# Attention scores from high and low parts of queries and keys, in a one-core hybrid decoder layer

## The chip, the core and the metric

The kernel runs on one NeuronCore of a Trainium2 chip. A core has engines that run their own instruction lists in order and wait for one another by semaphores: TensorE (PE, matrix products into PSUM), VectorE (DVE), ScalarE (ACT), GpSimd (POOL) and SyncE (SP, which here issues DMAs). A product has two records in the profile: the load of its stationary operand (PEld) and the product itself (PE). The metric is the device time of one execution, in microseconds (us); lower is better. The kernel before takes 1095.87 us (median of three runs, 1095.17 to 1096.69).

## The reference, cut to what matters

One layer of a decoder for 512 tokens of width 1024: a normalised input goes through three mixers side by side (a state-space mixer, dilated window attention, multi-scale pooling), then a gated sum, an output product and a squared-ReLU feed-forward part. All inputs are float32. The change is in the scores of the attention, of which the reference computes:

```python
# 3 groups of 4 heads, head size 128; group 0 dilation 1, groups 1 and 2 dilation 4 and 16
qh = _rms(q.reshape(b, S, ATTN_HEADS, ATTN_HEAD_DIM).astype(f32), q_norm_w)
kh = _rms(k.reshape(b, S, ATTN_HEADS, ATTN_HEAD_DIM).astype(f32), k_norm_w)
...
s = jnp.einsum('bhdnqe,bhdnke->bhdnqk', qb, kb) * (e ** -0.5)
...
s = jnp.where(valid, s + alibi[:, None, None], -jnp.inf)
lse = jax.nn.logsumexp(s, axis=-1)
```

## The kernel before

**Products.** Big products are not made with float32 operands. A float32 operand is cut into a high part, which ACT writes in the type float32r, and a low part, which DVE writes as the float32 value less the high part. A product is then three products of parts, summed in PSUM: `mm3` (lines 293 to 296) issues weight-high by x-low, weight-high by x-high, weight-low by x-high. `gemm_feat` and `gemm_tok` (lines 298 to 317) run `mm3` over eight blocks of the inner dimension and four accumulators. Their weights come through `wstream` (lines 283 to 291): SP loads a raw tile, ACT writes `wh` from it (line 279), DVE writes `wl` (line 280); four raw tiles and three `wh`, `wl` pairs are in turn.

**The scores.** `scores` (lines 578 to 644) does one group of four heads. For a head, `turn` transposes the four token blocks of queries and of keys on TensorE (lines 592 and 597) into one PSUM bank each, and ACT copies the two banks to `qT` and `kT` in SBUF, the keys scaled by `qkw` (lines 593 and 598). `score` multiplies them as float32 (line 613): four products a head, one for each block of 128 queries, against 128 keys (groups 1 and 2, and the first block of group 0) or 256 keys (the other three blocks of group 0). The profile shows two load and product records for each float32 product. DVE then scales and adds the position table (line 616) and takes maxima, ACT takes exponentials (line 628).

**Order.** The pieces of a group (turn of head 0; turn of head 1 and score of head 0; and so on) are put on a list, and `wstream` calls `tick` once per two blocks of a big product, which takes one piece off. So a head's turn and score stand between the products of the next projection. `flush` takes all pieces that are left at once. The `background` list adds, every second tick, one dot product of the adaLN weights on DVE (line 246) with its two loads on SP (line 240). A scheduler then orders each engine's list by its own estimate of times, with some work put ahead (`tc.high_priority`).

**Memory.** PSUM has eight banks, SBUF tiles of 128x512 come from 49 blocks. Both are handed out by `Slots` (lines 117 to 131): the block that was freed first is taken first, and an instruction that writes a block waits for the readers of its last use. A transposes' bank is free when ACT has copied it.

Of the kernel before, what the change touches and what calls it, by code (L numbers as in the profile page):

```python
# [10 lines left out]
F32 = mybir.dt.float32  # L11
F32R = mybir.dt.float32r
AF = mybir.ActivationFunctionType
ALU = mybir.AluOpType
# [3 lines left out]
P = 128  # L18
# [8 lines left out]
SOON = 200  # L27
# [71 lines left out]
def kernel(ctx: ExitStack, tc: tile.TileContext, a: dict, out: bass.AP, dbg=None):  # L99
    nc = tc.nc  # L100
# [16 lines left out]
    class Slots:  # L117
# [6 lines left out]
        def take(self, name, dt):  # L124
            i = self.idle.pop(0)
            t = self.pool.tile([P, T], dt, tag=f"{self.prefix}{i}", name=uid(name), bufs=1)
            self.used[id(t)] = (i, t)
            return t

        def free(self, t):  # L130
            self.idle.append(self.used.pop(id(t))[0])
# [3 lines left out]
    def blk(name, dt=F32):  # L135
        return sb.take(name, dt)
# [12 lines left out]
    def small(shape, name, bufs=1, dt=F32):  # L149
        return sm.tile(shape, dt, tag=name, name=uid(name), bufs=bufs)  # L150

    def psm(name="m"):
        return banks.take("ps" + name, F32)
# [8 lines left out]
    mm = nc.tensor.matmul  # L162
    V, S = nc.vector, nc.scalar
# [6 lines left out]
    def C(name):  # L170
        at, width = COFF[name]
        return cst[:, at : at + width]

    def table(name):
        at, width = COFF[name]
        t = [blk(name) for _ in range(width // T)]
        for i, x in enumerate(t):
            nc.gpsimd.dma_start(x, a["const"][:, at + i * T : at + (i + 1) * T])
        return t

    ident, tri = C("ident"), C("tri")
# [111 lines left out]
    def mm3(ps, wh, wl, xh, xl, first, last):  # L293
        mm(ps, lhsT=wh, rhs=xl, start=first, stop=False)  # L294
        mm(ps, lhsT=wh, rhs=xh, start=False, stop=False)  # L295
        mm(ps, lhsT=wl, rhs=xh, start=False, stop=last)  # L296
# [44 lines left out]
    with tc.manual_schedule(engines={E.DVE, E.Activation, E.PE, E.SP}):  # L341
# [107 lines left out]
        var, rt, r, t = (small([P, 4], "rx" + n) for n in "vryt")  # L449
# [24 lines left out]
        hl = [cpool.tile([P, T], F32R, name=f"hl{k}", tag=f"hl{k}") for k in range(8)]  # L474
# [31 lines left out]
        qkw = small([P, 1], "qkw")  # L506
# [54 lines left out]
    def take_k(ps):  # L561
        ks, rk = take(ps, "k")
        for tb in range(4):
            kv = ks[tb].rearrange("p (h e) -> p h e", h=4)
            with tc.high_priority(offset=SOON):
                V.tensor_tensor(kv, kv, rk[:, tb * 4 : tb * 4 + 4].unsqueeze(2).broadcast_to([P, 4, P]), ALU.mult)
        return ks
# [4 lines left out]
    def prob_ap(pt, gi, b):  # L572
        if gi == 0:
            n = P if b == 0 else 2 * P
            return pt[b // 2][:, (b % 2 + 1) * 2 * P - n : (b % 2 + 1) * 2 * P]
        return pt[0][:, b * P : (b + 1) * P]

    def scores(gi, qs, rq, ks):

        mx, zs = small([P, 16], f"mx{gi}"), small([P, 16], f"zs{gi}")  # L580
        nmx = small([P, 16], "nmx", 2)
        nkey = 2 * P if gi == 0 else P
        pr, turned, tab = [], {}, []

        def turn(h):
            if h == 0:
                tab.extend(table(f"al{gi}"))
            hs = slice(h * P, (h + 1) * P)
            qT, kT = blk("qT"), blk("kT")
            tp = psm("qT")  # L590
            for tb in range(4):
                nc.tensor.transpose(tp[:, tb * P : (tb + 1) * P], qs[tb][:, hs], ident)  # L592
            S.copy(qT, tp)  # L593
            free(tp)
            tp = psm("kT")
            for tb in range(4):
                nc.tensor.transpose(tp[:, tb * P : (tb + 1) * P], ks[tb][:, hs], ident)  # L597
            S.activation(kT, tp, AF.Copy, scale=qkw)
            free(tp)
            if h == 3:  # L600
                free(*qs, *ks)
            turned[h] = qT, kT

        def score(h):
            qT, kT = turned.pop(h)
            mxh = mx[:, h * 4 : h * 4 + 4]
            al = tab[h * nkey // T][:, h * nkey % T : h * nkey % T + nkey]
            pt = [blk("p") for _ in range(2 if gi == 0 else 1)]
            so, sp = [], [psm("S") for _ in pt]
            for b in range(4):  # L610
                n = prob_ap(pt, gi, b).shape[1]
                so.append(sp[0][:, b * P : (b + 1) * P] if gi else sp[b // 2][:, (b % 2 + 1) * 2 * P - n : (b % 2 + 1) * 2 * P])
                mm(so[b], lhsT=qT[:, b * P : (b + 1) * P], rhs=kT[:, (b + 1) * P - n : (b + 1) * P], start=True, stop=True)  # L613
            for b in range(4):
                ap = prob_ap(pt, gi, b)
                V.scalar_tensor_tensor(ap, so[b], rq[:, b * 4 + h : b * 4 + h + 1], al[:, nkey - ap.shape[1] :], ALU.mult, ALU.add)
                if gi == 0 and b < 2:
                    V.tensor_reduce(mxh[:, b : b + 1], ap, AX, ALU.max)
            free(*sp)
            if gi == 0:  # L620
                V.tensor_reduce(mxh[:, 2:4], pt[1].rearrange("p (b k) -> p b k", b=2), AX, ALU.max)
            else:
                V.tensor_reduce(mxh, pt[0].rearrange("p (b k) -> p b k", b=4), AX, ALU.max)
            nm = nmx[:, h * 4 : h * 4 + 4]
            V.tensor_scalar(nm, mxh, -1.0, None, ALU.mult)
            for b in range(4):
                ap = prob_ap(pt, gi, b)
                S.activation(ap, ap, AF.Exp, bias=nm[:, b : b + 1], accum_out=zs[:, h * 4 + b : h * 4 + b + 1])
            pr.append(pt)
            free(qT, kT)  # L630
            if h == 3:
                free(*tab)

        def piece(h):
            def go():
                if h < 4:
                    turn(h)
                if h > 0:
                    score(h - 1)
            return go  # L640

        probs.append(pr)
        stats.append((mx, zs))
        side.extend(piece(h) for h in range(5))
# [413 lines left out]
    with tc.issue_after(edgeV.ins), tc.issue_after(edgeS.ins):  # L1058
        qs, rq = take(qps, "q")
        ks = take_k(kps)  # L1060
# [3 lines left out]
    for gi in (1, 2):  # L1064
        if gi > 1:
            qps = gemm_tok(w_in, 8, Q + gi, rh, rl)
        qs, rq = take(qps, "q")
        kps = gemm_tok(w_in, 8, K + gi, rh, rl)
        ks = take_k(kps)
# [83 lines left out]
    with tc.manual_schedule(engines={E.DVE, E.Activation, E.PE}):  # L1153
# [61 lines left out]
        ta, tb = halves  # L1215
# [268 lines left out]
```

## Time and profile before

| What | Value |
|---|---|
| Median of three runs | 1095.87 us |
| Profiled execution | 1098.25 us |
| Its span | 1096.5 us, 14976 instructions |
| PE busy | 1087.1 us (99%), 5806 products |
| DVE busy | 717.4 us (65%) |
| ACT busy | 527.8 us (48%) |
| Granted TensorE clock | 1.0 |
| HBM traffic | 121 GB/s over the span |

The times in views are from the start of the span. In a timeline, a row is a run of like instructions on one engine: start, how long from the first start to the last end, engine, line, operation, output and inputs, shape, count. Products are pipelined: a product's record is longer than the time until the next one can start, so what a product costs in a dense row of products is the distance between starts. The chain of waits gives each piece of work only the time by which it held up the end.

### The profile page before, as it was taken

To read this page: it belongs to the slowest core of one execution; us is meant where nothing else is said; L and a number is where in the kernel's file an instruction comes from. 1 tells how busy PE (TensorE), PEld (TensorE's weight loads), DVE (VectorE), ACT (ScalarE), POOL (GpSimd) and SP (SyncE) were. 2 spreads that over 40 slices of the span, in tenths; PEclk is the share of its full clock that TensorE was granted. 3 is DMA by queue.
4 is the path that set the end of the run, shared out by engine and by line. 5 is a ranking of instruction groups with operands and counts; after the bars stand their busy time and mean duration, and the time that the engine had idled before them with its cause. 6 is when DMAs were issued, how large, how long until landed. Compare 5 with 4: busy or idle time off the path is not lost.

```text
span 1096.5 us, 14976 instructions
## 1 busy us (share of the span) xinstructions
PE 1087.1 (99%) x5806; PEld 927.0 (85%) x5806; DVE 717.4 (65%) x1383; ACT 527.8 (48%) x845; POOL 3.6 (0%) x10
## 2 busy tenths in 40 slices
PE   9999999999999999999999999999999999999998
PEld 7878888888887877888888888899889989989987
DVE  8975874582776778568843424577787587686664
ACT  8965875543695536625432123354344334335330
POOL 0000000000000000000000000000000000000000
PEclk9999999999999999999999999999999999999999
DMA  9853342443542354321232325360214224134032
GB/s 349 306 183 98 128 134 86 152 168 102 173 125 87 117 181 136 104 97 58 96 115 97 106 96 163 97 230 1 79 57 154 65 90 136 59 114 135 20 116 77
DMA packets 46666, 133.98 MB, mean 122 GB/s; under 512 B 5362, under 2 KB 6130, under 8 KB 46596
## 3 DMA queue, kind: packets, MB, share of 16 engines
q1 hardware_dynamic: 45392, 130.28, 36.0%
q0 software_dynamic: 480, 1.57, 0.5%
q10 hardware_dynamic: 724, 1.18, 0.3%
q8 instruction: 45, 0.74, 0.3%
q14 instruction: 25, 0.20, 0.1%
HBM read 130.89 MB, written 2.13 MB: 121 GB/s over the span
## 4 chain that ended last, share of the span: by engine, by line
PE 87%; ACT 4%; DVE 3%; DMA 3%; issue 1%; SPq 0%; ACTq 0%; DVEq 0%
PE psacc L294 22%; PE psacc L296 22%; PE psacc L295 22%; PE psacc L1345 11%; PE psacc L534 4%; DMA M<-prow 2%; PE psS L613 1%; DMA wa<-in_w_ada_dram 1%; DVE conv L850 1%; ACT wh L279 1%; PE pso L729 1%; PE pso L727 1%; DVE wl L280 1%; PE pskT L597 0%; PE psqT L592 0%
## 5 line engine op out<-in xcount | busy, mean ns | idle before, releaser
L280 DVE TENSOR_TENSOR wl<-raw,wh 128x1024 fp32r<-128x1024 f32 x140 | 171.0, 1222 | 192.2 <-ACT wh L279 190.9
L279 ACT CAST wh<-raw 128x1024 fp32r<-128x1024 f32 x140 | 146.8, 1050 | 241.1 <-PE psacc L295 168.8
L294 PE MATMUL psacc<-hl,wh 128*128 128x512 f32 x416 | 166.6, 401 | 3.4 <-DVE X L882 2.2
L295 PE MATMUL psacc<-hh,wh 128*128 128x512 f32 x416 | 162.1, 390 | 0.0
L296 PE MATMUL psacc<-hh,wl 128*128 128x512 f32 x416 | 162.0, 390 | 0.0
L295 PE MATMUL psacc<-ah,wh 128*128 128x512 f32 (+1 forms) x260 | 100.4, 386 | 0.0
L294 PE MATMUL psacc<-al,wh 128*128 128x512 f32 (+1 forms) x260 | 100.4, 386 | 0.0
L296 PE MATMUL psacc<-ah,wl 128*128 128x512 f32 (+1 forms) x260 | 100.3, 386 | 0.0
L294 PEld LDWEIGHTS psacc<-hl,wh 128*128 128x128 f32 x416 | 78.2, 188 | 21.7 <-DVE X L882 2.7
L295 PEld LDWEIGHTS psacc<-hh,wh 128*128 128x128 f32 x416 | 78.2, 188 | 16.9 <-issue 1.4
L296 PEld LDWEIGHTS psacc<-hh,wl 128*128 128x128 f32 x416 | 78.1, 188 | 16.7
L294 PE MATMUL psacc<-wl,rh 128*128 128x512 f32 x192 | 76.9, 401 | 0.0
L296 PE MATMUL psacc<-wh,rl 128*128 128x512 f32 x192 | 75.5, 393 | 0.0
L295 PE MATMUL psacc<-wh,rh 128*128 128x512 f32 x192 | 75.3, 392 | 0.0
L296 PEld LDWEIGHTS psacc<-ah,wl 128*128 128x128 f32 x260 | 48.8, 188 | 9.9
L294 PEld LDWEIGHTS psacc<-al,wh 128*128 128x128 f32 x260 | 48.9, 188 | 9.7
L295 PEld LDWEIGHTS psacc<-ah,wh 128*128 128x128 f32 x260 | 48.9, 188 | 9.6
L1405 DVE SCALAR_TENSOR_TENSOR xr<-psacc,modv,xr 128x512 f32<-128x512 f32 (+1 forms) x65 | 44.7, 739 | 18.6 <-PE psacc L296 18.6
L246 DVE SCALAR_TENSOR_TENSOR wa<-wa,crow 128x512 f32<-128x512 f32 x64 | 43.1, 688 | 20.0 <-DMA wa<-in_w_ada_dram 20.0
L296 PEld LDWEIGHTS psacc<-wh,rl 128*128 128x128 f32 x192 | 36.0, 188 | 7.6
L294 PEld LDWEIGHTS psacc<-wl,rh 128*128 128x128 f32 x192 | 36.1, 188 | 7.3 <-ACT qT L593 0.2
L295 PEld LDWEIGHTS psacc<-wh,rh 128*128 128x128 f32 x192 | 36.1, 188 | 7.0
(408 smaller groups left out, 2360.8 us busy)
## 6 DMA issues: line engine op xcount, KB each, us to landing
raw<-in_w_in_dram SPq DMA_DIRECT2D x80, 512.0 KB, 3.5
raw<-in_w_ff_dram SPq DMA_DIRECT2D x52, 512.0 KB, 3.7
wa<-in_w_ada_dram SPq DMA_DIRECT2D x64, 256.0 KB, 3.6
wada<-in_w_ada_dram SPq DMA_DIRECT2D x14, 512.0 KB, 7.8
rawl<-in_w_ff_dram SPq DMA_DIRECT2D x12, 512.0 KB, 3.5
wst<-in_w_in_dram SPq DMA_DIRECT2D x16, 256.0 KB, 7.8
M<-prow SPq DMA_DIRECT2D x16, 256.0 KB, 3.8
raw<-in_w_ssd_out_dram SPq DMA_DIRECT2D x8, 512.0 KB, 3.5
```

The lines of the kernel that those rows point to most:

```text
L246: V.scalar_tensor_tensor(wa[i], wa[i], 1.0, crow[i], ALU.mult, ALU.mult, accum_out=d[:, i : i + 1])
L279: S.copy(wh, raw)
L280: V.tensor_tensor(wl, raw, wh.bitcast(F32), ALU.subtract)
L294: mm(ps, lhsT=wh, rhs=xl, start=first, stop=False)
L295: mm(ps, lhsT=wh, rhs=xh, start=False, stop=False)
L296: mm(ps, lhsT=wl, rhs=xh, start=False, stop=last)
L534: mm(ps[j], lhsT=t[:, j, :], rhs=w, start=first, stop=last)
L613: mm(so[b], lhsT=qT[:, b * P : (b + 1) * P], rhs=kT[:, (b + 1) * P - n : (b + 1) * P], start=True, stop=True)
L727: mm(od, lhsT=vs[kb][:, hs], rhs=pT[b // 2][:, cs : cs + P], start=(b == 0), stop=False, skip_group_check=True)
L729: mm(ov[:, b, :], lhsT=vs[b][:, hs], rhs=pT[0][:, b * P : (b + 1) * P], start=False, stop=(gi == 2 and b == 3), skip_group_check=True)
L1345: mm(o, lhsT=x[:, cs], rhs=y, start=first and k == 0 and j == 0 and n == 0, stop=k == 3 and n == 2, skip_group_check=True)
L1405: V.scalar_tensor_tensor(xT[d][:, ts], p[:, : ts.stop - ts.start], modv[:, 3, d : d + 1], xT[d][:, ts], ALU.mult, ALU.add)
```

## The change

Query and key banks leave by two instructions each: ACT writes the high part in float32r (the query's copy becomes an activation with scale 1.0), and DVE writes the low part, reading the same PSUM bank and the high part. Both are put ahead in the order. Each score block is now `mm3`: three products of parts in place of one float32 product. A head holds four SBUF blocks (`qTh`, `qTl`, `kTh`, `kTl`) in place of two.

```diff
-            qT, kT = blk("qT"), blk("kT")
-            tp = psm("qT")
-            for tb in range(4):
-                nc.tensor.transpose(tp[:, tb * P : (tb + 1) * P], qs[tb][:, hs], ident)
-            S.copy(qT, tp)
-            free(tp)
-            tp = psm("kT")
-            for tb in range(4):
-                nc.tensor.transpose(tp[:, tb * P : (tb + 1) * P], ks[tb][:, hs], ident)
-            S.activation(kT, tp, AF.Copy, scale=qkw)
-            free(tp)
+            qT, kT = ([blk(n + p, F32R) for p in "hl"] for n in ("qT", "kT"))
+            for t, xs, sc in ((qT, qs, 1.0), (kT, ks, qkw)):
+                tp = psm("qT" if xs is qs else "kT")
+                for tb in range(4):
+                    nc.tensor.transpose(tp[:, tb * P : (tb + 1) * P], xs[tb][:, hs], ident)
+                with tc.high_priority(offset=SOON):
+                    S.activation(t[0], tp, AF.Copy, scale=sc)
+                    V.scalar_tensor_tensor(t[1], tp, sc, t[0].bitcast(F32), ALU.mult, ALU.subtract)
+                free(tp)
...
-                mm(so[b], lhsT=qT[:, b * P : (b + 1) * P], rhs=kT[:, (b + 1) * P - n : (b + 1) * P], start=True, stop=True)
+                mm3(so[b], *(t[:, b * P : (b + 1) * P] for t in qT), *(t[:, (b + 1) * P - n : (b + 1) * P] for t in kT), True, True)
...
-            free(qT, kT)
+            free(*qT, *kT)
```

The lines behind the change move up by two, so line 616 of before is line 614 after.

Three places show what the change moves. First PE, at the score of head 0 of group 0 (`psS` is the scores' bank, `kT` moves and `qT` is stationary). Before:

```order
L597 MATMUL pskT_1134<-cst,k_715 128x128
L613 MATMUL psS_1142<-kT_1074,qT_1073 128x128
L613 MATMUL psS_1142<-kT_1074,qT_1073 128x256
L613 MATMUL psS_1143<-kT_1074,qT_1073 128x256 x2
L294 MATMUL psacc_996<-wl_1163,rh_265 128x512
```

And of the change:

```order
L593 MATMUL pskT_1141<-cst,k_715 128x128
L294 MATMUL psS_1150<-kTl_1076,qTh_1073 128x128
L295 MATMUL psS_1150<-kTh_1075,qTh_1073 128x128
L296 MATMUL psS_1150<-kTh_1075,qTl_1074 128x128
L294 MATMUL psS_1150<-kTl_1076,qTh_1073 128x256
L295 MATMUL psS_1150<-kTh_1075,qTh_1073 128x256
L296 MATMUL psS_1150<-kTh_1075,qTl_1074 128x256
L294 MATMUL psS_1151<-kTl_1076,qTh_1073 128x256
L295 MATMUL psS_1151<-kTh_1075,qTh_1073 128x256
```

Four products become twelve; the place between the transposes and the next projection's products is the same.

Second, PE behind the last turn of group 1, where a new projection begins (`psacc` are its accumulators; what each waits for stands in brackets). Before:

```order
L613 MATMUL psS_1549<-kT_1475,qT_1474 128x128 x3
L294 MATMUL psacc_1604<-wl_1611,rh_262 128x512 [waits DVE_49]
L295 MATMUL psacc_1604<-wh_1610,rh_262 128x512
L296 MATMUL psacc_1604<-wh_1610,rl_67_266 128x512
L294 MATMUL psacc_1605<-wl_1611,rh_262 128x512 [waits Activation_49]
L295 MATMUL psacc_1605<-wh_1610,rh_262 128x512
L296 MATMUL psacc_1605<-wh_1610,rl_67_266 128x512
L294 MATMUL psacc_1606<-wl_1611,rh_262 128x512 [waits Activation_49]
```

And of the change:

```order
L296 MATMUL psS_1629<-kTh_1540,qTl_1539 128x128
L294 MATMUL psacc_1692<-wl_1699,rh_262 128x512 [waits DVE_49]
L295 MATMUL psacc_1692<-wh_1698,rh_262 128x512
L296 MATMUL psacc_1692<-wh_1698,rl_67_266 128x512
L294 MATMUL psacc_1693<-wl_1699,rh_262 128x512 [waits DVE_49]
L295 MATMUL psacc_1693<-wh_1698,rh_262 128x512
L296 MATMUL psacc_1693<-wh_1698,rl_67_266 128x512
L294 MATMUL psacc_1694<-wl_1699,rh_262 128x512 [waits DVE_49]
```

The second and third accumulators take the two banks of the transposes just before. They waited for ACT, which had copied these banks; they now wait for DVE, which reads them after ACT.

Third, DVE at the same place. Before, from the low part of one weight tile (`wl`) to the next:

```order
L280 TENSOR_TENSOR wl_1657<-raw_1654,wh_1656 128x1024
L616 SCALAR_TENSOR_TENSOR p_1488<-psS_1489,rqy_988,al_317_1359 128x128 x4
L623 TENSOR_REDUCE mx_307_1322<-p_1488 128x4
L625 TENSOR_SCALAR nmx_1324<-mx_307_1322 128x4
L280 TENSOR_TENSOR wl_1696<-raw_1693,wh_1695 128x1024
L616 SCALAR_TENSOR_TENSOR p_1548<-psS_1549,rqy_988,al_317_1359 128x128 x4
```

And of the change, from behind the like `nmx` row:

```order
L623 TENSOR_SCALAR nmx_1372<-mx_315_1370 128x4
L246 SCALAR_TENSOR_TENSOR wa_1780,dot_1784<-wa_1780,crow_81 128x512
L246 SCALAR_TENSOR_TENSOR wa_1781,dot_1784<-wa_1781,crow_81 128x512
L248 TENSOR_TENSOR modv_94<-dot_1784 128x1
L256 TENSOR_TENSOR modv_94<-modv_94,vec_79 128x1
L557 TENSOR_REDUCE ssq_1669<-sq_1670 128x4
L280 TENSOR_TENSOR wl_1792<-raw_1789,wh_1791 128x1024
L596 SCALAR_TENSOR_TENSOR qTl_1611<-psqT_1614,qTh_1610 128x512
L596 SCALAR_TENSOR_TENSOR kTl_1613<-pskT_1621,qkw_282,kTh_1612 128x512
L614 SCALAR_TENSOR_TENSOR p_1628<-psS_1629,rqy_988,al_325_1407 128x128 x4
```

A whole adaLN dot product (two `wa` rows, which need their loads) and a square sum now stand between `nmx` and `wl`, and the two low parts between `wl` and the scores' row. Further ahead, on PE, 5 products of a projection stood between the query transposes of head 0 of group 1 and its first key transpose; now 19 do.

## The prediction

> **What bounds the kernel.** The page first: how busy each engine is.
>
> ```profile
> span 1096.5 us, 14976 instructions
> PE 1087.1 (99%) x5806; PEld 927.0 (85%) x5806; DVE 717.4 (65%) x1383; ACT 527.8 (48%) x845; POOL 3.6 (0%) x10
> PE 87%; ACT 4%; DVE 3%; DMA 3%; issue 1%; SPq 0%; ACTq 0%; DVEq 0%
> ```
>
> PE is busy 99% of the span and makes 87% of the chain of waits, so TensorE sets the end. Two things can move the time: how long its products take, and anything that makes its list wait. DVE and ACT matter only where PE waits for them. The change lies between 95 and 215 us; the same stretch cut in three, with the engines' busy time (PE, PEld, DVE, ACT):
>
> ```profile
> 95.00:115.00 20.00, 20.00 (x106) 16.99 (x104) 7.03 (x13) 10.03 (x20) 0.00 (x0) 1.00 0.26 81
> 115.00:132.00 17.00, 17.00 (x89) 13.77 (x88) 16.81 (x45) 13.84 (x33) 0.00 (x0) 1.00 0.35 112
> 132.00:215.00 83.00, 83.00 (x425) 70.14 (x424) 49.83 (x133) 50.81 (x121) 1.61 (x3) 1.00 0.41 131
> ```
>
> PE has no free time in any of them, at a granted clock of 1.00. DVE has 73.7 of 120 us busy, but 16.81 of 17.00 between 115 and 132, where the heads of group 0 are flushed.
>
> **Term 1: the score products.** What they cost now stands in the chain of waits, one row a head; the first is of group 0, the second of group 1:
>
> ```profile
> 105.89 1.52 PE psS L613 x8
> 132.37 0.89 PE psS L613 x8
> ```
>
> The eight records are four float32 products, two passes each. Four heads at 1.52 and eight at 0.89 are 13.2 us, all on the path. What replaces them are 144 products of float32r parts: 4 heads x 3 blocks x 3 = 36 with 256 keys and 108 with 128 keys. For 256 columns the trace has the same product in the feed-forward part, and for 512 in the projections:
>
> ```profile
> 818.58 0.28 PE L1345 MATMUL psacc<-gl,wh 128*128 128x256 f32 x1
> 818.70 0.28 PE L1345 MATMUL psacc<-gh,wh 128*128 128x256 f32 x1
> 640.12 0.39 PE L294 MATMUL psacc<-pooll,wh 128*128 128x512 f32 x1
> 640.35 0.39 PE L295 MATMUL psacc<-poolh,wh 128*128 128x512 f32 x1
> ```
>
> So 0.120 us for 256 columns and 0.23 for 512 (0.227 over many): 36 x 0.120 = 4.3 us. **No float32r product with 128 columns is in the trace**, and three quarters of the new ones are that. Bounds. From 512 to 256 columns 0.107 us go, so 128 columns alone would be 0.120 - 0.053 = 0.067; then 108 x 0.067 + 4.3 = 11.5 us, 1.7 less than now. The other end is that a short float32r product keeps the two passes of a float32 one: 2 x 0.112 = 0.224, in all 28.5 us, 15.3 more. Between them stands the load of the stationary operand, which each product has. Products of one single column show what a load costs when nothing streams:
>
> ```profile
> 11.15 1.05 PE L412 MATMUL pssx<-ones,sq 128*128 128x1 f32 x8
> L412 PE MATMUL pssx<-ones,sq x16: 250/250/271, 8.4 to 11.9; 128*128 128x1 f32 x16
> L412 PEld LDWEIGHTS pssx<-ones,sq x16: 186/192/192, 8.4 to 11.9; 128*128 128x128 f32 x16
> L1345 PEld LDWEIGHTS psacc<-gl,wh x144: 188/192/192, 818.0 to 1045.8; 128*128 128x128 f32 x144
> ```
>
> Eight such products take (1.05 - 0.25) / 7 = 0.114 us each, and a float32 pass of 128 columns 0.89 / 8 = 0.111. The load records of float32 and float32r are alike, 192 ns. I take 0.112, the row nearest in kind: 108 x 0.112 = 12.1, with the 256-column ones 16.4 us. Term 1 is 16.4 - 13.2 = **+3.2 us** (+3.1 at 0.111, +4.1 at the 0.120 of 256 columns). It splits: group 0 gains 0.1 a head, groups 1 and 2 lose 12 x 0.112 - 0.89 = 0.45 a head. Three thin products pay three loads where two were paid.
>
> [...]
>
> **Term 2: work on DVE and ACT.** The same low-part instruction is in the pooling mixer (line 1000), and the same scaled high part (line 999); beside them the copy that goes:
>
> ```profile
> L1000 DVE SCALAR_TENSOR_TENSOR pooll<-psmix,vec,poolh x8: 743/746/750, 533.4 to 553.9; 128x512 fp32r<-128x512 f32 x8
> L999 ACT ACTIVATE poolh<-psmix,vec x8: 676/688/720, 532.5 to 552.7; 128x512 fp32r<-128x512 f32 x8
> L593 ACT COPY qT<-psqT x12: 566/580/606, 99.7 to 198.8; 128x512 f32<-128x512 f32 x12
> ```
>
> DVE gets 24 x 0.746 = 17.9 us, ACT 12 x (0.688 - 0.580) = 1.3 us. In total both fit the 45 us that each has free between 95 and 215 us: no cost by amount. The cost is in who waits.
>
> **Term 3: new waits of PE.** The bank of a transpose was free when ACT had copied it, now when DVE has read it too. The next projection's accumulators take these very banks. Before, at the start of the projection behind group 1 (PE, ACT, DVE; then two rows of the list of waits, the adaLN loads' time to landing, and from the chain the exchange of softmax statistics):
>
> ```profile
> 147.51 0.48 PE L294 MATMUL psacc<-wl,rh 128*128 128x512 f32 x1
> 148.29 0.47 PE L294 MATMUL psacc<-wl,rh 128*128 128x512 f32 x1
> 148.60 0.39 PE L295 MATMUL psacc<-wh,rh 128*128 128x512 f32 x1
> 147.59 0.61 ACT L593 COPY qT<-psqT 128x512 f32<-128x512 f32 x1
> 147.25 1.23 DVE L280 TENSOR_TENSOR wl<-raw,wh 128x1024 fp32r<-128x1024 f32 x1 [4.16 <-ACT wh L279]
> PEld psacc L294 <- ACT qT L593: 0.2, 1, 0.2
> DVE wa L246 <- DMA wa<-in_w_ada_dram: 20.0, 14, 4.1
> wa<-in_w_ada_dram SPq DMA_DIRECT2D x64, 256.0 KB, 3.6
> 219.11 0.89 PE psmzN L654 x8
> ```
>
> Already now the second accumulator waits for ACT (148.29 to 148.60 is 0.31, not 0.227; a wait of 0.2 on the list). ACT is done at 148.2. After, DVE must follow: the weight tile's low part in front ends at 148.5, `qTl` adds 0.75, so the bank is free at 149.2, while PE comes at 148.29 + 0.45 of longer scores = 148.7: **0.5 us**, if DVE is on time. It need not be: in its new order an adaLN dot product stands in front, and such rows have waited for their loads 14 times, 20.0 us in all, up to 4.1, with 3.6 from issue to landing. Everything behind `psacc_1693` on PE's list stands still meanwhile, and on DVE the scores' rows and maxima behind `kTl`. I take 2 us here (0.5 to 4). The same handover comes behind group 2's third turn, with `wl` behind the low parts instead of ahead: 1 us (0 to 2). Between 115 and 132 us DVE has 0.2 us free and gets five low parts by the first score of group 1, 3.7 us; the scheduler has put 14 projection products (3.2 us) more between that group's first query and key transposes, so most is covered; 1 us (0 to 3). The last exchange of softmax statistics on PE, at 219 us, waits for the DVE rows behind all this: 0.3 (0 to 2). Term 3: **+4.3 us**, from 0.5 to 11. Four blocks for a head instead of two also shift which SBUF block each adaLN load takes; this is in the spread.
>
> **Sum.** On the profiled execution (1098.25 us, 2.4 above the median of the runs): 1098.25 + 3.2 + 4.3 = 1105.8. Against the median: 1095.87 + 7.5, **1103.4 us**.
>
> **Rivals.**
> - *Loads hide (not slower).* If a 128-column product costs under (13.2 - 4.3) / 108 = 0.082 us, term 1 turns negative; at 0.067, and with DVE on time, the time is 1095.87 - 1.7 + 0.5 = 1094.7. For it: loads overlap products in every dense row. Against: 0.114 with nothing to stream. [...] Chance 8%.
> - *Two passes stay.* At 0.224 the time is 1095.87 + 15.3 + 1, as slower PE gives DVE time: 1112. The two passes belong to float32 operands; the 256-column float32r rows show one record per product, so I see little for it. Chance 5%.
> - *DVE is on time everywhere.* Only term 1 and 0.5: 1099.6. It asks that the scheduler's order fits the real times; at 148 us it misses by a little. Chance 15%.
> - *DVE falls behind and stays behind.* Waits for adaLN loads push the low parts at each handover, 11 us: 1110. Chance 12%.
>
> **How the numbers follow.** The forecast (waits of 2 to 9 us) has 60%. The range leaves out the two-pass rival and the hidden loads and takes in the rest: 1098.5 to 1110. About 0.2% (2.2 us) is what a measurement of this kernel can tell from no change. Faster by that needs hidden loads and something more: 3%. Within it, the rest of that rival and a little: 7%. Slower: 90%.
>
> **What would show it.** Right: score rows of about 1.4 us a head in group 0 and 1.34 in groups 1 and 2 in the chain; PE waits on the low parts of line 596 by accumulators, longest near 150 us; DVE up by 18 us. Wrong: 128-column starts 0.07 or 0.22 apart (term 1); no PE wait on line 596 (term 3); a wait that is longest somewhere else, or a longer stretch behind 230 us, where I expect none.

## The result, and the profile after

The changed kernel takes **1110.1 us** (median of four runs, 1107.69 to 1110.53) against 1095.91 for the kernel before beside it: a ratio of 1.0125, 95% interval 1.0109 to 1.0140, or 13.7 us (11.9 to 15.3). The forecast was 1103.4, in a range that ended at 1110.0, so the median lies 0.1 us beyond its end. The sign was right; the loss is almost twice as large as forecast. The profiled execution took 1110.26 us, 12.0 more than the profiled one of before; its page:

```profile
span 1108.2 us, 15109 instructions
PE 1095.1 (99%) x5854; PEld 934.2 (84%) x5854; DVE 731.8 (66%) x1407; ACT 527.8 (48%) x845; POOL 3.6 (0%) x10
```

The share of PE is the same 99%, so the page alone hides what happened: a slower product counts as busy too (6.72 of 7.00 us at a clock of 0.56, in the third row). The stretches show it (columns as before: PE, PEld, DVE, ACT, POOL, then the granted clock):

```profile
115.00:132.00 17.00, 16.77 (x94) 13.82 (x93) 16.72 (x41) 14.03 (x36) 0.47 (x1) 1.00 0.43 140
132.00:215.00 83.00, 79.77 (x407) 67.12 (x406) 54.52 (x131) 47.35 (x109) 1.61 (x3) 0.96 0.38 118
152.00:159.00 7.00, 6.72 (x17) 5.32 (x18) 6.69 (x20) 4.52 (x13) 0.00 (x0) 0.56 0.49 150
228.00:234.00 6.00, 6.00 (x28) 5.16 (x29) 5.54 (x33) 0.53 (x4) 0.00 (x0) 0.72 0.47 134
```

Between 132 and 215 us PE now stands still for 3.2 us, and in two short stretches its clock is 0.56 and 0.72 on average, where it was 1.00 in the same stretches before. TensorE's timeline shows the two effects together (start, duration, what it waited for; here and below, rows that lie between those shown are left out):

```profile
149.36 0.40 PE L296 MATMUL psacc<-wh,rl 128*128 128x512 f32 x1
152.28 0.80 PE L294 MATMUL psacc<-wl,rh 128*128 128x512 f32 x1 [2.53 <-DVE qTl L596]
152.88 0.63 PE L295 MATMUL psacc<-wh,rh 128*128 128x512 f32 x1
...
158.00 0.50 PE L295 MATMUL psacc<-wh,rh 128*128 128x512 f32 x1
158.34 0.39 PE L296 MATMUL psacc<-wh,rl 128*128 128x512 f32 x1
```

The list of waits names the releasers of the longest new ones (total, times, longest):

```profile
PE psacc L294 <- DVE qTl L596: 2.7, 2, 2.5
PE psmzN L652 <- issue: 1.4, 1, 1.4
PE psacc L294 <- DVE p L614: 0.7, 1, 0.7
```

PE waits 2.53 us for the bank of `qTl`, where the prediction put its longest wait. Behind it the products start 0.427 us apart instead of 0.227: from 152.88 to 158.34 there are 13 steps in 5.46 us, which would have been 2.95, so **2.5 us** are lost at half clock. The same happens from 230.3 to 233.6 us behind the exchange of softmax statistics (`psmzN`): 8 steps in 3.3 us, 1.5 lost. The prediction has no such term, and it expected nothing behind 230 us.

The products themselves: from the first transpose of a head's keys to the first product behind its scores, a head of group 0 and one of group 1, in the kernel before and then in the changed one:

```profile
105.29 0.60 PE L597 MATMUL pskT<-cst,k 128*128 128x128 f32 x4
107.06 0.58 PE L294 MATMUL psacc<-wl,rh 128*128 128x512 f32 x1
131.77 0.60 PE L597 MATMUL pskT<-cst,k 128*128 128x128 f32 x4
132.20 1.06 PE L613 MATMUL psS<-kT,qT 128*128 128x128 f32 x8
133.02 0.48 PE L294 MATMUL psacc<-wl,rh 128*128 128x512 f32 x1
```

```profile
105.11 0.60 PE L593 MATMUL pskT<-cst,k 128*128 128x128 f32 x4
106.96 0.40 PE L294 MATMUL psacc<-wl,rh 128*128 128x512 f32 x1
139.40 0.60 PE L593 MATMUL pskT<-cst,k 128*128 128x128 f32 x4
140.02 0.27 PE L296 MATMUL psS<-kTh,qTl 128*128 128x128 f32 x1
140.13 0.28 PE L294 MATMUL psS<-kTl,qTh 128*128 128x128 f32 x1
140.24 0.28 PE L295 MATMUL psS<-kTh,qTh 128*128 128x128 f32 x1
141.13 0.45 PE L294 MATMUL psacc<-wl,rh 128*128 128x512 f32 x1
```

Group 0 goes from 1.77 to 1.85 us a head, group 1 from 1.25 to 1.73: 4 x 0.08 + 8 x 0.48 = **4.2 us** for all twelve heads. The 128-column products start 0.11 us apart, as the prediction took them.

So the profile gives: products 4.2, new waits 2.5 + 1.4 + 0.7, half clock 2.5 + 1.5, together 12.8 where the two profiled executions lie 12.0 apart: a wait of 2.2 us that before had at 431 us has gone (its row stands in the last section), and some short ones are new, the longest of 1.1 us at 426 us.

### The profile page after: what moved, and what is told of

Its sections match the earlier page's. It is cut to its first block, busy times and chain, and to the rows that moved or that the text cites. A ratio compares the mean times of both kernels' runs of the same rounds, so it can differ in the third digit from the quotient of the medians.

```text
span 1108.2 us, 15109 instructions
## 1 busy us (share of the span) xinstructions
PE 1095.1 (99%) x5854; PEld 934.2 (84%) x5854; DVE 731.8 (66%) x1407; ACT 527.8 (48%) x845; POOL 3.6 (0%) x10
## 4 chain that ended last, share of the span: by engine, by line
PE 71%; ACT 2%; DVE 1%; DMA 1%; issue 0%; SPq 0%; ACTq 0%; DVEq 0%
PE psacc L294 19%; PE psacc L295 18%; PE psacc L296 18%; PE psacc L1343 11%; DMA wa<-in_w_ada_dram 1%; PE pso L727 1%; PE psy L930 1%; PE pso L725 1%; ACT wh L279 1%; DVE conv L848 1%; PE psyo L938 0%; DVE wl L280 0%; PE psst L889 0%; PE psmix L294 0%; PE psmix L296 0%; PE psmix L295 0%
```

## The experiments

Each run is compared with runs of the kernel before on the same chip (medians 1096.09, 1096.79 and 1095.61 in the three sets of experiments, 1095.91 for the changed kernel). The column "us more" is the ratio less one, times 1096; by the intervals it is known to 1 to 2.4 us, so rows that lie closer than about 2 us can't be told apart by it.

| Run | Median, us | Ratio, 95% interval | us more |
|---|---|---|---|
| changed kernel | 1110.10 | 1.0125 (1.0109 to 1.0140) | 13.7 |
| products_only | 1107.37 | 1.0097 (1.0083 to 1.0111) | 10.6 |
| lows_only | 1097.42 | 1.0015 (1.0006 to 1.0024) | 1.6 |
| lows_long | 1101.27 | 1.0038 (1.0026 to 1.0050) | 4.2 |
| g1_products | 1103.61 | 1.0069 (1.0047 to 1.0091) | 7.6 |
| g2_products | 1104.08 | 1.0069 (1.0055 to 1.0083) | 7.6 |
| ada_held | 1109.38 | 1.0119 (1.0103 to 1.0134) | 13.0 |
| exps_later | 1105.13 | 1.0086 (1.0073 to 1.0099) | 9.4 |
| order_mended | 1101.87 | 1.0047 (1.0034 to 1.0060) | 5.2 |
| before_held | 1096.00 | 0.9995 (0.9987 to 1.0004) | -0.5 |
| filled_wait | 1107.47 | 1.0104 (1.0090 to 1.0117) | 11.4 |
| filled_a_third | 1110.07 | 1.0119 (1.0101 to 1.0137) | 13.0 |

### The two halves of the change: products_only, lows_only

```diff
# products_only: no low part; high parts in all three products
-                    V.scalar_tensor_tensor(t[1], tp, sc, t[0].bitcast(F32), ALU.mult, ALU.subtract)
-                mm3(so[b], *(t[:, b * P : (b + 1) * P] for t in qT), ...
+                mm3(so[b], *[qT[0][:, b * P : (b + 1) * P]] * 2, ...
# lows_only: float32 copies as before, low parts on DVE, float32 products
-                mm3(so[b], ...
+                mm(so[b], lhsT=qT[0][:, b * P : (b + 1) * P], rhs=kT[0][...], start=True, stop=True)
```

> The change without its low parts: ACT's high part alone empties a transpose's bank, and each score block is three float32r products of high parts (low parts are left out). Theory (products cost 3.2 us, the rest of the loss is PE waiting for DVE at bank handovers and a halved clock behind the two longest waits): 3 us above before, 1098 to 1100, no PE wait on line 596, granted clock 1.00 throughout. Rival (the float32r score products themselves bring the loss, by their loads or by lowering the clock): 8 us or more above before, with stretches at half clock between 100 and 235 us.

> The low parts without the new products: ACT copies float32 as before, DVE computes a low part from each bank, the scores are the float32 products of before and read no low part. Theory: the whole loss but the 3.2 us of the products, so 1103 to 1108, with a PE wait on a low part near 150 us that is 0.4 us longer than after's 2.5 (PE arrives earlier) and products 0.43 us apart behind it. Rival: DVE's added 18 us are hidden, within 3 us of before, no half clock.

**The theory of both expectations fell here.** It gave DVE's low parts 4 us and more and the products 3. Measured: the low parts alone cost 1.6 us, the products alone 10.6. In products_only a transposes' bank is emptied by ACT alone and no score product reads a low part, and yet PE waits near the same places. Its list of waits:

```profile
PE psacc L294 <- DVE p L613: 2.8, 2, 2.1
PE psmzN L651 <- issue: 2.0, 1, 2.0
```

The 2.1 us are near 154 us, now for the bank of a score. Behind it the first two products start 0.54 us apart (154.05, 154.59), and the mean clock is 0.997 in three of the four runs and 1.000 in the one of 1104.64 us. The scores' row `p` on DVE is late there with two adaLN dots ahead of it that had waited 0.34 and 0.84 us for their loads. In lows_only DVE does all its added work, and PE passes the handover near 150 us with hardly a wait (0.1 us more than a product takes), by its timeline:

```profile
149.00 0.40 PE L296 MATMUL psacc<-wh,rl 128*128 128x512 f32 x1
149.36 0.50 PE L294 MATMUL psacc<-wl,rh 128*128 128x512 f32 x1
```

What differs between lows_only and the changed kernel is above all ACT's list. First lows_only, then the changed kernel, in the same stretch:

```profile
144.23 0.59 ACT L331 COPY q<-psacc 128x512 f32<-128x512 f32 x1 [1.53 <-PE psacc L296]
146.33 1.06 ACT L279 CAST wh<-raw 128x1024 fp32r<-128x1024 f32 x1
147.28 0.61 ACT L595 ACTIVATE qTh<-psqT 128x512 f32<-128x512 f32 x1
148.80 0.44 ACT L626 ACTIVATE p<-p,nmx 128x128 f32<-128x128 f32 x1
```

```profile
145.70 0.40 ACT L626 ACTIVATE p<-p,nmx 128x128 f32<-128x128 f32 x1 [2.29 <-DVE nmx L623]
146.87 0.56 ACT L331 COPY q<-psacc 128x512 f32<-128x512 f32 x1
149.21 1.04 ACT L279 CAST wh<-raw 128x1024 fp32r<-128x1024 f32 x1
150.15 0.60 ACT L595 ACTIVATE qTh<-psqT 128x512 fp32r<-128x512 f32 x1
```

In lows_only the copies of the finished accumulators, the next weight tile's `wh` and `qTh` (here a float32 copy) come first and the exponentials (`p`) behind them. In the changed kernel the exponentials come first, and ACT stands 2.29 us for the maximum from DVE (`nmx`); everything behind is 3 us later (`qTh` at 150.15 against 147.28), while PE's transposes are later by 0.6 us (146.69 against 146.07).

The exponentials in front are not new, though. In the kernel before ACT stands for the maximum in the same way:

```profile
143.19 0.40 ACT L628 ACTIVATE p<-p,nmx 128x128 f32<-128x128 f32 x1 [2.24 <-DVE nmx L625]
```

But there DVE makes the maximum at 142.92 us, and `qT` starts 1.8 us behind its transposes on PE (147.59 against 145.83). In the changed kernel it does so at 145.49, with two low parts ahead of the scores' row on DVE (142.36 to 143.62), and `qTh` starts 3.5 us behind. So it is lows_only that has another order on ACT than before. On DVE the changed kernel has two dots between the maximum and the next `wl` that wait for their loads:

```profile
146.83 0.69 DVE L246 SCALAR_TENSOR_TENSOR wa<-wa,crow 128x512 f32<-128x512 f32 x1 [1.17 <-DMA wa<-in_w_ada_dram]
148.81 0.69 DVE L246 SCALAR_TENSOR_TENSOR wa<-wa,crow 128x512 f32<-128x512 f32 x1 [1.28 <-DMA wa<-in_w_ada_dram]
```

A new theory: the waits come from the **order** in which the scheduler lays out the lists of ACT and DVE around these heads, and not from the low parts holding banks as such.

### Order or amount: lows_long

```diff
# lows_only, and in groups 1 and 2 every second block's product issued twice
+                for _ in range(2 if gi and b % 2 else 1):
                     mm(so[b], lhsT=qT[0][:, b * P : (b + 1) * P], rhs=kT[0][...], start=True, stop=True)
```

> All low parts as in the changed kernel, float32 products in the scores, and in groups 1 and 2 the products of every second block issued twice: TensorE then spends 12 x 0.111 = 1.34 us a head there, as with three products of parts, 3.6 us more than with the low parts alone, at the same work on DVE and ACT. Theory (the long waits come from the order in which the lists of ACT and DVE are laid out when the products are in parts, not from the amount of work): low parts alone, 1097.4, + 3.6 = 1101 (1100 to 1102.5), no PE wait over 1 us between 145 and 235 us. Rival (longer products and 18 us more on DVE together make DVE late): PE waits of 2 us near 150 us and 1.5 near 228 as in the changed kernel, half clock behind them, 1107 to 1111.

It came out at 1101.27, with the expected 1101, and no wait of PE in the stretch is over 0.3 us. The longest wait on its list is an old one behind the attention, 1.6 us for `X`.

Here DVE and ACT have the work of the changed kernel, and TensorE as much to do in groups 1 and 2. The waits don't come; ACT's list has the exponentials behind the copies, as in lows_only. **Amount alone is excluded.** What is left is the order, or that the scores read the low parts; but in products_only no score reads one, and PE waits.

### Which group: g1_products, g2_products

```diff
# parts in one group only (g1_products: gi == 1; g2_products: gi == 2), else lows_only
+                if gi == 1:
                     mm3(so[b], ...
+                else:
+                    mm(so[b], lhsT=qT[0][:, b * P : (b + 1) * P], rhs=kT[0][...], start=True, stop=True)
```

> Three products of parts in group 1 alone; groups 0 and 2 have float32 products (their low parts are computed and not read). Theory (each group's products change the lists around its own heads): the wait near 150 us is there, 2 to 2.7 us with 2 to 3 us lost at half clock behind it, those near 208 and 228 are gone: 1097.4 + 4 x 0.45 + 4.5 to 5.5 = 1103.5 to 1105. Rival (lateness adds up over all groups): with a third of the products the wait near 150 us falls under 1.5 us and no half clock follows, 1099 to 1101.

> Three products of parts in group 2 alone; groups 0 and 1 have float32 products (their low parts are computed and not read). Theory (each group's products change the lists around its own heads): no wait over 0.5 us near 150 us, waits of 0.5 to 1.2 us near 204 and 1 to 2 us at the exchange near 222 us: 1097.4 + 1.8 + 2 to 3, and 1.5 more if the clock halves behind the exchange: 1101 to 1104. Rival (the waits belong to whatever comes last and add up): a wait near 150 us as in the changed kernel.

The longest wait between 145 and 235 us, from the list of waits of g1_products:

```profile
PE psacc L294 <- DVE qTl L596: 1.7, 1, 1.7
```

And from that of g2_products:

```profile
PE psmzN L655 <- issue: 1.3, 1, 1.3
```

With parts in group 1 alone the wait near 150 us is there, and ACT has the exponentials in front (its first copy of an accumulator starts at 146.5 us, against 146.9 in the changed kernel and 144.2 in lows_only); with parts in group 2 alone there is none at that place, ACT has them behind, and the exchange waits. By the medians the costs add up: 1.6 for the low parts, 6.0 for each group's products beyond that, 13.6 in all, and the changed kernel has 13.7. With intervals of 1.5 to 2.4 us on the two rows so close a fit is luck; it fits that group 0, whose products have become hardly longer, costs little. Two expectations missed. The exchange waits 1.0 us in g1_products too, where none was expected. And the profiled run of g1_products has the wait near 150 us (1.7 us, less than the 2 to 2.7 expected) but no half clock behind it (the products start 0.23 us apart); its six runs go from 1101.23 to 1110.66. That comes back below.

### Which part of the order: ada_held, exps_later, order_mended, before_held

```diff
# ada_held: no dot while the scores of groups 1 and 2 are on the list, made up behind them
-        if ticks[0] % 2 == 0 and background:
-            background.pop(0)()
+        if hold[0]:
+            owed[0] += ticks[0] % 2 == 0
+        elif background and (ticks[0] % 2 == 0 or owed[0]):
+            owed[0] -= ticks[0] % 2
+            background.pop(0)()
# exps_later: a head's exponentials two pieces later, behind the last accumulator copy on ACT
+                if h > 2:
+                    expo(h - 3)
...
+            with tc.issue_after(copied[0].ins):
+                for b in range(4):
                     S.activation(ap, ap, AF.Exp, bias=nm[:, b : b + 1], accum_out=...)
# order_mended: both, with the hold one projection longer; before_held: that hold in the kernel before
```

> The changed kernel with the adaLN dot products held back while the scores of groups 1 and 2 are under way, and made up behind them. Theory (the dots' loads made DVE late for the bank near 150 us): the wait there falls from 2.5 us to 0.5 to 1, the half clock behind it goes, and the exchange near 228 us finds DVE on time: 1102 to 1105. Rival (DVE is late by the amount of its work, not by the loads it waits for): the wait near 150 us stays at 2 us or more, time within 2 us of after.

ada_held stems from the first theory still. The wait near 150 us was still 2.0 us, and its time is that of the changed kernel: with the dots gone DVE waited 3.7 us for ACT instead. The dots made up behind group 2 now stood ahead of the exchange, whose wait grew to 2.4.

> The changed kernel with only one half of order_mended: a head's exponentials are issued two pieces later and behind the copies of the projection's accumulators on ACT; the adaLN dots stay where they are. Theory (both stand ahead of what PE needs near 150 us, the exponentials on ACT and the dots on DVE): about half of the wait near 150 us stays (1 to 2 us, DVE late by its dots), the wait at the exchange near 228 us goes under 1 us, so 1102 to 1106. Rival (the exponentials alone are the cause): as order_mended, 1101 to 1102, no wait over 1 us. Rival (they don't matter): as the changed kernel, 1108 to 1111.

> The changed kernel with all its products and low parts, in another order: a head's exponentials are issued two pieces later and behind the copies of the projection's accumulators on ACT, and the adaLN dot products are held back until behind group 2's scores (made up later). To be read against before_held, which has the same hold. Theory (exponentials and dots that wait stand ahead of the copies, weight parts and low parts that PE needs): no PE wait over 1 us between 145 and 235 us, no half clock, 3.2 us of products and 1 to 2 us of short waits above before_held. Rival (the waits belong to the products and low parts in any order): 9 us or more above before_held, with half clock.

> The kernel before, with the adaLN dot products held back until behind group 2's scores. Theory (before has hardly a wait at these handovers, 0.1 to 0.3 us each, and its longer waits, near 252, 337 and 431 us, lie behind): 0 to 3 us faster than before, 1093 to 1096, by what the moved dots do to those three. Rival (made up later, the dots make new waits there): 1097 or more.

With the exponentials moved alone, ACT is on time (`qTh` at 148.52), but DVE is not. Its rows in exps_later:

```profile
147.36 0.69 DVE L246 SCALAR_TENSOR_TENSOR wa<-wa,crow 128x512 f32<-128x512 f32 x1 [1.12 <-DMA wa<-in_w_ada_dram]
149.35 0.69 DVE L246 SCALAR_TENSOR_TENSOR wa<-wa,crow 128x512 f32<-128x512 f32 x1 [1.28 <-DMA wa<-in_w_ada_dram]
150.95 1.22 DVE L280 TENSOR_TENSOR wl<-raw,wh 128x1024 fp32r<-128x1024 f32 x1
152.08 0.69 DVE L598 SCALAR_TENSOR_TENSOR qTl<-psqT,qTh 128x512 fp32r<-128x512 f32 x1
```

Two dots wait for their loads, 1.12 and 1.28 us, ahead of `wl` and `qTl`, and PE waits 2.4 us (more than the 1 to 2 expected); the wait at the exchange is gone from the list, but the mean clock is still 0.998 in all four runs. So near 150 us two late lists stand side by side, ACT by its exponentials and DVE by its dots, and mending one leaves the other. With both moved, nothing near 150 us is over 1 us, and the clock is 1.00 in every stretch read from 100 to 235 us. The waits of order_mended in the stretch:

```profile
PE psacc L297 <- DVE p L619: 0.6, 1, 0.6
PE psS L297 <- DVE p L619: 0.3, 1, 0.3
PE psacc L297 <- DVE qTl L601: 0.2, 1, 0.2
```

order_mended is 5.7 us above before_held by the table: 4.2 of products, and the short waits listed are 1.1 of the other 1.5. The hold alone does nothing measurable to the kernel before. All products and low parts are in order_mended, so about 8 of the 13.7 us go away with another order. It is still slower than the kernel before, and nothing here beats that.

### The half clock: filled_wait, filled_a_third

```diff
# in the projection behind group 1: n = 3 (filled_wait) or 1 (filled_a_third)
+                for _ in range(again if k == j == 0 else 0):
+                    mm3(ps[j], th[:, j, :], tl[:, j, :], wh, wl, True, True)
                 mm3(ps[j], th[:, j, :], tl[:, j, :], wh, wl, k == 0, k == nk - 1)
```

> The changed kernel; in the projection behind group 1 the first accumulator's first three products are issued four times (each time from a cleared bank), so that 9 more products of 0.227 us, 2.0 us in all, stand in the 2.6 us in which PE waited near 150 us; DVE and SP keep their order. Theory (an idle PE halves the clock behind it): the bank comes free at the same time, the wait left is 0.6 us, the 14 products behind it start 0.227 instead of 0.427 us apart: 2.9 us less than after, 1106.5 to 1108. Rival (the clock falls for another reason, the work before it, or a fixed time): products behind the wait still 0.427 apart, time within 0.5 us of after.

> As filled_wait, with 3 instead of 9 additional products (0.68 us) in the wait near 150 us, which leaves about 1.9 us of it. If the clock halves by the length of the wait alone: between after (half clock, 1110) and filled_wait (none, 1107.5) at one value in all runs. If it is judged over fixed stretches of time in which the wait may fall in one or two: runs spread between these two, some with and some without the half clock, as g1_products did (1101.2 to 1110.7).

With nine more products in the wait, the kernel does more work and its row is 2.3 us lower, with intervals that overlap (9.9 to 12.8 against 11.9 to 15.3). The clock says more: its mean is 0.999 or 1.000 in all four runs, where the changed kernel has 0.995 in three runs and 0.998 in one. In filled_wait's timeline of TensorE the wait left is 0.46 us, and the products behind it start 0.23 us apart:

```profile
153.29 0.50 PE L294 MATMUL psacc<-wl,rh 128*128 128x512 f32 x1 [0.46 <-DVE qTl L598]
153.63 0.39 PE L295 MATMUL psacc<-wh,rh 128*128 128x512 f32 x1
153.86 0.40 PE L296 MATMUL psacc<-wh,rl 128*128 128x512 f32 x1
```

So near 150 us the half clock went with the idle time, 2.53 us of it against 0.46, and not with the work before it. The mean of the profiled run is 1.000, so the exchange, too, has full speed behind it, which the added products don't explain. With three more products, in filled_a_third, 1.84 us of wait stay:

```profile
152.62 0.63 PE L294 MATMUL psacc<-wl,rh 128*128 128x512 f32 x1 [1.84 <-DVE qTl L598]
153.05 0.63 PE L295 MATMUL psacc<-wh,rh 128*128 128x512 f32 x1
...
156.37 0.39 PE L294 MATMUL psacc<-wl,rh 128*128 128x512 f32 x1
```

Its five runs go from 1104.60 (mean clock 1.000) to 1110.76 (0.996): the same kernel with and without half clock. They are spread as the second expectation has it, and not at one value as the first, which speaks against a length of wait alone; fixed stretches of time themselves no run shows, and how long PE waited in the runs that were not profiled isn't known.

## Why the prediction was right in sign and short by half

- **Term 1, the products.** The price of a product was right: 128-column products 0.11 us apart, 256-column 0.12. That the load sets this fits the 0.114 of the one-column products, but no run tried it apart. The term was mis-sized: 4.2 us, not 3.2. The rows of the chain, 1.52 and 0.89, were taken as what a head's float32 products occupy. From their first start to the next product they occupy 1.34 (105.72 to 107.06) and 0.82 (132.20 to 133.02). So group 0 lost 0.08 a head instead of gaining 0.1, which is most of the difference. The rivals of hidden loads and of two passes both fell.
- **Term 2, amount.** Nearly right. DVE rose by 14.4 us (717.4 to 731.8), not 17.9, and ACT by nothing. The low parts alone cost 1.6 us (0.7 to 2.6), which the term put at nothing; lows_long shows that the amount brings none of the long waits.
- **Term 3, the waits.** This is the step that failed: "The bank of a transpose was free when ACT had copied it, now when DVE has read it too." The places were right (near 150 us, the third turn of group 2, the exchange). The sum was close too, 4.6 us of new waits against 4.3, but partly by luck: the exchange waits 1.4 us where 0.3 was forecast, and from 115 to 132 us PE stands 0.2 us where 1 was. The cause was not right. That DVE reads the bank isn't enough: with the low parts alone the loss is 1.6 us and there is no wait near 150; without any low part PE waits all the same; and with all of them in another order (order_mended) the longest wait there is 0.6 us. The releaser in the row, `qTl`, was only the last of a late list: ACT had stood 2.29 us for a maximum with the copies and `wh` behind its exponentials, and DVE 1.17 and 1.28 us for adaLN loads. The prediction did see the dot ahead of `qTl`, as something that adds to the wait; it never asked what stands ahead on ACT, whose term it had closed with +1.3 us.
- **The half clock** is the missing term: 4.0 us in the profile, behind the two longest of the new waits. With it the "longer stretch behind 230 us, where I expect none" came too.
- **The rivals.** "DVE is on time everywhere" (1099.6) is about what order_mended and lows_long do, 1101 to 1102. "DVE falls behind" named the right figure, 1110, and one of the two late lists, but the figure is luck: its price was all waits, where in the profile 4.0 of the 8.6 us beyond the products are clock.

What stays open: why the scheduler puts the exponentials behind the copies with low parts and float32 products (lows_only, lows_long, g2_products near 150 us), and in front of them with products in parts, as in the kernel before. That its estimate of the products' time is the reason would fit, but was not tried. How much of the late maximum is due to the low parts ahead of it, in this order, was not measured apart. How the 8 us divide between the exponentials and the dots can't be said either, since each alone leaves the wait near 150 us.

## What to carry to other kernels

The releaser that a wait names is the last of its list: before a cause is written down, look at what stood ahead of it on that engine and of what released it, and run each half of the change alone, since here the row names the low parts, which alone cost 1.6 us. Compare the order of the lists with the kernel before and with each half: on lists laid out by a scheduler a change can move work on engines that it does not touch. And read the granted clock behind a wait of TensorE: here 2.5 us were lost at half clock behind a wait of 2.53 us, and none behind one of 2.22 us in the kernel before.

## What the runs showed of the hardware that was not expected

Waits of PE of 1.2 us (filled_a_third, at the exchange), 1.4 us (changed kernel, there too), 1.84 us (filled_a_third near 150 us) and 2.53 us (changed kernel near 150 us) were followed by half clock: products of 512 columns then start 0.427 us apart instead of 0.227. It needn't come: in the kernel before a wait of 2.22 us has full speed behind it:

```profile
431.01 0.50 PE L294 MATMUL psacc<-hl,wh 128*128 128x512 f32 x1 [2.22 <-DVE X L882]
431.35 0.40 PE L295 MATMUL psacc<-hh,wh 128*128 128x512 f32 x1
```

Read in windows of 0.4 us, the granted clock of the changed kernel is 1.00 or 0.50 from 146 to 160 and from 225 to 236 us, but for the windows in which it changes. It is 0.50 from 151.4 to 158.2 us and from 229.9 to 233.3 us, so it fell while PE still waited in the first case and 2 us after PE had resumed in the second. The first stretch is 6.8 us long, behind a wait of 2.53 us, and the second 3.4, behind one of 1.41. In filled_a_third the products behind the wait of 1.84 us come 0.43 us apart until about 156.2 us. What decides whether a wait is followed by half clock, and for how long, no run shows. The six runs of g1_products go from 1101.23 us at a mean clock of 1.000 to 1110.66 at 0.995.
